# A two-block transformer kernel: who adds the experts' rows, who sums the squares, and the order of the modulation weights

## The chip, the cores and the metric

The kernel runs on one core of one Trainium2 chip. The metric is the device time of one execution in microseconds; three runs of the kernel before gave 2313.27, 2318.12 and 2326.68 us, so the median is 2318.12. The engines are called as in the profile: PE (TensorE's matmuls; PEld is its weight loads), DVE (VectorE), ACT (ScalarE), POOL (GpSimd) and SP (SyncE, which issues most DMAs).

## The reference

A sequence of 256 latent tokens and 256 context tokens, 1024 wide, goes through two blocks in float32. The first block has two layers. Each modulates the tokens, runs a mixer (an even one with neighbourhood attention and an mLSTM, then an odd one with grouped-query attention), adds its output to the residual `x`, and then runs 16 experts of which each token uses two:

```python
comb = (one_hot(e_idx, N_EXPERTS) * w[..., None]).sum(axis=1)
for e in range(N_EXPERTS):
    y = y + comb[:, e:e + 1] * ((silu(h @ w1[e]) * (h @ w3[e])) @ w2[e])
x = x + g2 * y                       # g2: a gate of the modulation
# the next layer begins with
h = x * rsqrt(mean(x * x) + EPS) * g * (1 + scale) + shift
# where shift, scale and gates are silu(c) @ ada_w[l] + ada_b[l]
```

In the first layer the experts run on all 512 tokens, in the second on the 256 latent tokens alone. The second block is two layers of a hybrid of attention and convolutions with a feed-forward part, on the latent tokens.

## The kernel before

The residual is kept feature-major: `xl` (latent) and `xc` (context) are tiles of 128 partitions x 8 groups (`k`) of features x 256 tokens. Every large product is made from three matmuls of halves: a weight tile `raw` is rounded on ACT into `wh` (L90), DVE subtracts to get `wl` (L91), and PE runs `wh` and `wl` against the halves of the input (L105 to L107). There are three buffers each for `wh` and `wl`, and eight for `raw`. SP loads the weights in the order in which the program asks for them.

**The end of an expert layer (`moe`, from L1689).** Each expert works on the up to 128 tokens that chose it. Experts 0 to 13 scatter their weighted rows to a DRAM tensor `yd` with one row for each token and choice (L1671, a DMA from POOL). When expert 14 has gone up, `rows_back` (L1692) loads these rows: for each block `t` of 128 tokens two tiles `g[0]`, `g[1]` in `raw` buffers, four blocks in the first layer and two in the second. Behind the last expert DVE adds each pair (L1732); an order written by hand (`issue_after`) puts these adds behind the last weight subtract, and the last one behind the last split of an expert's output. The outputs of experts 14 and 15 (`LATE` = 2) stay in SBUF as halves `yh`, `yl`. PE then builds for each `k` a bank of 256 or 512 tokens: matmuls of `yh`, `yl` with a selection matrix `which` (`late_sum`, L1743) and of the added rows with the identity, which transposes them (`first_sum`, L1737). DVE multiplies the bank by the gate and adds it to the residual (L1763), once for each `k` and segment: 16 instructions in the first layer, 8 in the second.

**The squares.** `Stats` collects the sum of squares of each token of the residual. In the first expert layer ACT squares two `k` of a segment at a time (`gather`, L187), DVE adds the squares of the pairs onto each other (L189) and the two halves of the result (L204), and PE sums over the partitions with a column of ones into `tot` (`settle`, L206). It settles twice: once when `k` = 5 is done, once at the end. The second expert layer only notes the tiles (`gather_later`), and the next block does the work. `Stats.add` (L213) is a method that no caller uses here: it squares on ACT and lets PE sum each square for itself; its tiles `sq` have three buffers. `Stats.rstd` (L228) takes mean and epsilon on DVE (L233), the power -0.5 on POOL (L168), and spreads the reciprocals over the partitions by matmuls with the identity (L239, "the spread").

**The next stage (`odd_mixer`, L1779).** It calls `rstd`, modulates both segments (L891 on DVE, L901 on ACT, L902 on DVE) and runs the first projection, `lin_tok` on four chunks of weights. Between chunks `c.between` is called, which runs one step of `ada`: matmuls of the second layer's modulation weights (L824) into a bank of the same PSUM pool as `tot`.

**Held splits.** `c.held` is a list from which `split_w` takes one entry at a time: the ACT cast and the DVE subtract of that weight tile are queued behind the two instructions of the entry. At the end of the first expert layer the first next tile is held behind the last row add and the last rounding of an expert's output (`c.early`), the two after it behind the last half add of squares and the last square. The order within each engine is otherwise made by a scheduler from priorities, when the program is built.

Of the kernel before, what the change touches and what calls it, by code (L numbers as in the profile page):

```python
# [170 lines left out]
class Stats:  # L171
# [41 lines left out]
    def add(self, i, x):  # L213

        c, nc = self.c, self.c.nc
        _, n, w = x.shape
        sq = c.const.tile([P, 512], F32, name="sq", tag="sq", bufs=3)
        sv = sq[:, :n * w].rearrange("p (n w) -> p n w", n=n)
        nc.scalar.activation(sv, x, AF.Square)
        for k in range(n):  # L220
            for t in range(w // P):
                left = self.left.get(i + t, KD) - 1
                nc.tensor.matmul(self.tot[:, i + t:i + t + 1], sv[:, k, t * P:(t + 1) * P], c.ones[:, 0:1],
                                 start=self.fresh, stop=left == 0, skip_group_check=True)
                self.fresh = False
                self.left[i + t] = left

    def rstd(self, i, n=1):  # L228

        c, nc = self.c, self.c.nc  # L230
        assert not any(self.left[i + j] for j in range(2 * n))
        r = c.const.tile([P, 4], F32, name="rstd", tag="rstd", bufs=2)
        nc.vector.tensor_scalar(r[:, :2 * n], self.tot[:, i:i + 2 * n], 1.0 / D, EPS, op0=ALU.mult, op1=ALU.add)  # L233
        c.rsqrt_small(r[:, :2 * n], r[:, :2 * n], 2 * n)
        outs = []
        for a in range(n):
            out = c.ps("rstd")
            for t in range(2):
                nc.tensor.matmul(out[:, t * P:(t + 1) * P], r[:, 2 * a + t:2 * a + t + 1].to_broadcast((P, P)), c.ident,  # L239
                                 start=True, stop=True, skip_group_check=True)  # L240
            outs.append(out[:, :256])
        return outs

# [1160 lines left out]
def moe(c, s, L, segs, mods, routes, yd, later, slots, late, more=()):  # L1404
# [287 lines left out]
    def rows_back():  # L1692

        for t in range(nt):
            g = []
            for k in range(2):
                g.append(c.raw().rearrange("p a b -> p (a b)"))
                nc.sync.dma_start(g[k], rows[t, :, k])
            gs.append(g)

    x, f = (xh, xl), None
# [25 lines left out]
                                            op0=ALU.add, op1=ALU.is_equal)  # L1727
    ys.append(down(NE - 1, *end))
    ys = ys[NE - LATE:]
    for g in gs:  # L1730
        with tc.issue_after(done[1].ins if g is gs[-1] else c.splits[-1]):
            added = nc.vector.tensor_tensor(g[0], g[0], g[1], op=ALU.add).ins  # L1732
    c.early = added, c.last_h

    def first_sum(k, ts):
        for t in ts:
# [11 lines left out]
    with tc.issue_after(done[0].ins):  # L1748
# [6 lines left out]
        for k in range(KD):  # L1755
# [4 lines left out]
            late_sum(k, (LATE - 1,))  # L1760
            ps = banks[k]
            for i, (x, r) in enumerate(segs):
                nc.vector.scalar_tensor_tensor(x[:, k, :], ps[:, 256 * i:256 * i + 256], mods.col(5, k, r), x[:, k, :],  # L1763
                                               op0=ALU.mult, op1=ALU.add)
            if k % 2:
                for i, (x, r) in enumerate(segs):
                    if later:
                        st.gather_later(x[:, k - 1:k + 1, :])
                    else:
                        place = spare([P, 512], F32, "sqs")  # L1770
                        q = st.gather(x[:, k - 1:k + 1, :], 2 * i, place)
                if k == KD - 3 and not later:
                    st.settle()
    if not later:
        c.held = [(st.settle().ins, q.ins)] * 2 + [c.early]
    return st


def odd_mixer(c, s, xl, xc, st, mods, A, B, ada):  # L1779
# [61 lines left out]
        nc.vector.tensor_tensor(B[:, :n, 1::2], x[:, :, 0::2], bc(tab[:, P + 1::2]), op=ALU.mult)  # L1841
        nc.vector.tensor_tensor(dst, A[:, :n], B[:, :n], op=ALU.add)

    c.between = lambda: ada(1)
    banks = [c.acc() for _ in range(4)]
    c.lin_tok(h, W[:, 1024:1536], 512, range(4), banks)
    for t in range(4):
        nc.scalar.copy(v[:, t, :], banks[t][:, 256:512])
        heads(banks[t][:, 0:256].rearrange("p (h d) -> p h d", d=P), 2, 1, t - 2 if t >= 2 else None, kk[:, t])
# [290 lines left out]
```

## Time and profile before

| | |
|---|---|
| median of three runs | 2318.12 us |
| profiled execution | 2316.98 us |
| its span | 2315.2 us |
| PE / PEld busy | 2222.4 us (96%) / 1887.8 us (82%) |
| DVE / ACT / POOL busy | 1789.7 us (77%) / 1505.2 us (65%) / 152.3 us (7%) |
| bytes moved by DMA | 507.24 MB |

The profile is one execution. Busy is the time in which an engine had an instruction running; a matmul's end is modelled, so a busy PE is not one at its peak. Instructions of one engine overlap a little in the records, so that steps are somewhat shorter than durations. PE's clock column is the share of full speed that was granted (1.00 is 2.4 GHz, 0.50 is 1.2 GHz). A wait is idle time of an engine in front of an instruction, with what released it.

### The profile page before, as it was taken

How to read it: one execution, taken by the hardware profiler on the slowest of the kernel's cores; microseconds unless marked ns; L12 is line 12 of the kernel's file. 1: busy time of each engine (PE TensorE's matmuls, PEld its weight loads, DVE VectorE, ACT ScalarE, POOL GpSimd, SP SyncE). 2: the span in 40 equal slices, each digit the busy share in tenths (PEclk: the TensorE clock that was granted, in tenths of full speed). 3: DMA queues.
4: the chain of work that ended last, by engine and by line, in shares of the span. 5: the costliest groups of instructions: out<-in, count | busy, mean ns of one | idle time of the engine just before them, and what ended most of it. 6: DMA issues, size and time to landing. Idle time of an engine off the chain costs nothing.

```text
span 2315.2 us, 37957 instructions
## 1 busy us (share of the span) xinstructions
PE 2222.4 (96%) x14089; PEld 1887.8 (82%) x14089; DVE 1789.7 (77%) x2817; ACT 1505.2 (65%) x2398; POOL 152.3 (7%) x202
## 2 busy tenths in 40 slices
PE   8999999889999998999999999999999999999999
PEld 5665657767777667777778899999999899999997
DVE  4334743789989775899888999778976899867984
ACT  4333442478877453788776999656765999755773
POOL 0020000111110100111101100000000100000000
PEclk9999979899999999999999999999999999999999
DMA  8577603899993745999946545656666645656653
GB/s 303 170 242 279 204 26 118 312 347 366 365 336 142 270 167 207 377 398 348 325 148 204 177 136 150 190 182 183 194 201 185 184 139 146 186 178 183 192 184 117
DMA packets 206204, 507.24 MB, mean 219 GB/s; under 512 B 22711, under 2 KB 32335, under 8 KB 206008
## 3 DMA queue, kind: packets, MB, share of 16 engines
q1 hardware_dynamic: 196728, 490.08, 63.1%
q0 software_dynamic: 9280, 14.62, 1.7%
q8 instruction: 114, 1.87, 0.3%
q14 instruction: 82, 0.67, 0.1%
HBM read 498.39 MB, written 25.19 MB: 226 GB/s over the span
## 4 chain that ended last, share of the span: by engine, by line
PE 51%; DVE 10%; issue 8%; ACT 6%; DMA 3%; POOL 1%; DVEq 0%; SPq 0%; ACTq 0%; POOLq 0%
PE acc L106 15%; PE acc L107 15%; PE acc L105 14%; DVE wl L91 6%; ACT wh L90 3%; PE ps L164 2%; ACT cp L592 1%; DMA raw<-in_exp_w 1%; DMA rawm<-in_exp_w 1%; PE ps L1903 1%; DMA rawr<-in_exp_w 1%; ACT mtf L1635 1%; PE ps L451 0%; PE acc L1894 0%; DVE conf L597 0%
## 5 line engine op out<-in xcount | busy, mean ns | idle before, releaser
L91 DVE TENSOR_TENSOR wl<-raw,wh 128x1024 fp32r<-128x1024 f32 (+2 forms) x520 | 616.1, 1191 | 240.8 <-ACT wh L90 236.4
L90 ACT CAST wh<-raw 128x1024 fp32r<-128x1024 f32 (+2 forms) x520 | 532.1, 1026 | 356.1 <-PE acc L106 187.4
L106 PE MATMUL acc<-hl,wh 128*128 128x256 f32 (+1 forms) x1568 | 450.0, 287 | 0.3 <-DVE hl L916 0.3
L107 PE MATMUL acc<-hh,wl 128*128 128x256 f32 (+1 forms) x1568 | 450.0, 287 | 0.0
L105 PE MATMUL acc<-hh,wh 128*128 128x256 f32 (+1 forms) x1568 | 449.1, 287 | 0.7 <-ACT hh L913 0.6
L105 PEld LDWEIGHTS acc<-hh,wh 128*128 128x128 f32 x1568 | 295.5, 189 | 11.7 <-issue 4.2
L106 PEld LDWEIGHTS acc<-hl,wh 128*128 128x128 f32 x1568 | 295.9, 189 | 7.0 <-issue 2.5
L107 PEld LDWEIGHTS acc<-hh,wl 128*128 128x128 f32 x1568 | 294.9, 188 | 5.8 <-issue 1.3
L91 DVE TENSOR_TENSOR wl<-rawm,wh 128x1024 fp32r<-128x1024 f32 x210 | 250.9, 1219 | 17.6 <-ACT wh L90 14.2
L90 ACT CAST wh<-rawm 128x1024 fp32r<-128x1024 f32 x210 | 218.1, 1052 | 48.8 <-PE acc L107 45.9
L106 PE MATMUL acc<-wl,xh 128*128 128x512 f32 x512 | 211.5, 413 | 16.4 <-DVE wl L91 16.1
L105 PE MATMUL acc<-wh,xh 128*128 128x512 f32 x512 | 202.0, 399 | 6.3 <-PEq L1328 6.3
L107 PE MATMUL acc<-wh,xl 128*128 128x512 f32 x512 | 202.5, 395 | 0.0
L105 PE MATMUL acc<-bh,wh 128*128 128x256 f32 x640 | 178.6, 279 | 0.7 <-ACT bh L273 0.7
L106 PE MATMUL acc<-bl,wh 128*128 128x256 f32 x640 | 178.7, 279 | 0.4 <-DVE bl L274 0.4
L107 PE MATMUL acc<-bh,wl 128*128 128x256 f32 x640 | 178.7, 279 | 0.0
L592 ACT ACTIVATE cp<-ap,col 128x256 f32<-128x256 f32 x368 | 164.7, 506 | 6.4 <-DVE conf L597 6.4
L106 PE MATMUL acc<-wl,hh 128*128 128x512 f32 (+1 forms) x384 | 145.4, 379 | 2.2 <-DVE wl L91 1.9
L105 PE MATMUL acc<-wh,hh 128*128 128x512 f32 (+1 forms) x384 | 147.1, 383 | 0.0
L106 PEld LDWEIGHTS acc<-wl,xh 128*128 128x128 f32 x512 | 97.1, 190 | 60.6 <-DVE wl L91 41.0
L107 PE MATMUL acc<-wh,hl 128*128 128x512 f32 (+1 forms) x384 | 144.6, 377 | 0.0
L106 PEld LDWEIGHTS acc<-bl,wh 128*128 128x128 f32 x640 | 121.1, 189 | 0.8 <-DVE bl L274 0.8
(493 smaller groups left out, 4514.4 us busy)
## 6 DMA issues: line engine op xcount, KB each, us to landing
rawm<-in_exp_w SPq DMA_DIRECT2D x210, 512.0 KB, 6.9
raw<-in_w_in SPq DMA_DIRECT2D x152, 512.0 KB, 3.6
raw<-in_exp_w SPq DMA_DIRECT2D x96, 512.0 KB, 7.0
raw<-in_ada_w SPq DMA_DIRECT2D x80, 512.0 KB, 5.1
raw<-in_w_up SPq DMA_DIRECT2D x80, 512.0 KB, 3.7
rawr<-in_exp_w SPq DMA_DIRECT2D x66, 512.0 KB, 7.0
raw<-in_w_down SPq DMA_DIRECT2D x44, 512.0 KB, 4.4
raw<-in_even_w_in SPq DMA_DIRECT2D x24, 512.0 KB, 5.1
```

What stands on the lines that cost most here:

```text
L90: nc.scalar.copy(h[:, :, :n], raw[:, :, :n])
L91: self.splits.append(nc.vector.tensor_tensor(l[:, :, :n], raw[:, :, :n], h[:, :, :n], op=ALU.subtract).ins)
L105: nc.tensor.matmul(out, a[0], b[0], start=start, stop=False, skip_group_check=True)
L106: nc.tensor.matmul(out, a[0], b[1], start=False, stop=False, skip_group_check=True)
L107: return nc.tensor.matmul(out, a[1], b[0], start=False, stop=stop, skip_group_check=True)
L164: self.nc.tensor.transpose(out, in_, self.ident[:n, :n])
L592: nc.scalar.activation(p[:, i, :], src[:, i, :], AF.Copy, scale=wv)
L1635: nc.scalar.activation(v, a, AF.Tanh, scale=0.5)
L1903: nc.tensor.matmul(po[:, :256], v[:, b, g0 * P:(g0 + 1) * P], pT[:, b].rearrange("p t q -> p (t q)"), start=b == 0, stop=b == 3)
```

## The change

The row pairs are added on POOL, in `rows_back`, right behind the loads of each pair, with no order by hand. The entry `c.early` names the last split of an expert's output in place of the last row add. In the first expert layer `Stats.add` takes the place of `gather` and `settle`: after each `k`, each segment is squared on ACT (128x256) and two matmuls sum it into `tot`, so there are 32 of these matmuls where there were 8. The two held tiles are now queued behind the last update of the residual and the last square. And the modulation steps that run between the four chunks of the first projection are queued on PE behind the last matmul of the spread.

```diff
@@ Stats.add
-        nc.scalar.activation(sv, x, AF.Square)
+        last = nc.scalar.activation(sv, x, AF.Square).ins
...
+        return last
@@ Stats.rstd
-                nc.tensor.matmul(out[:, t * P:(t + 1) * P], r[:, 2 * a + t:2 * a + t + 1].to_broadcast((P, P)), c.ident,
-                                 start=True, stop=True, skip_group_check=True)
+                self.spread = nc.tensor.matmul(out[:, t * P:(t + 1) * P],
+                                               r[:, 2 * a + t:2 * a + t + 1].to_broadcast((P, P)), c.ident,
+                                               start=True, stop=True, skip_group_check=True).ins
@@ moe, rows_back
                 nc.sync.dma_start(g[k], rows[t, :, k])
+            nc.gpsimd.tensor_tensor(g[0], g[0], g[1], op=ALU.add)
             gs.append(g)
@@ moe, behind the last expert
-    for g in gs:
-        with tc.issue_after(done[1].ins if g is gs[-1] else c.splits[-1]):
-            added = nc.vector.tensor_tensor(g[0], g[0], g[1], op=ALU.add).ins
-    c.early = added, c.last_h
+    c.early = done[1].ins, c.last_h
@@ moe, for each k
-                nc.vector.scalar_tensor_tensor(x[:, k, :], ps[:, 256 * i:256 * i + 256], mods.col(5, k, r), x[:, k, :],
-                                               op0=ALU.mult, op1=ALU.add)
-            if k % 2:
-                for i, (x, r) in enumerate(segs):
-                    if later:
-                        st.gather_later(x[:, k - 1:k + 1, :])
-                    else:
-                        place = spare([P, 512], F32, "sqs")
-                        q = st.gather(x[:, k - 1:k + 1, :], 2 * i, place)
-                if k == KD - 3 and not later:
-                    st.settle()
+                last = nc.vector.scalar_tensor_tensor(x[:, k, :], ps[:, 256 * i:256 * i + 256], mods.col(5, k, r),
+                                                      x[:, k, :], op0=ALU.mult, op1=ALU.add).ins
+            for i, (x, r) in enumerate(segs):
+                if not later:
+                    q = st.add(2 * i, x[:, k:k + 1, :])
+                elif k % 2:
+                    st.gather_later(x[:, k - 1:k + 1, :])
     if not later:
-        c.held = [(st.settle().ins, q.ins)] * 2 + [c.early]
+        c.held = [(last, q)] * 2 + [c.early]
@@ odd_mixer
-    c.between = lambda: ada(1)
+    def behind():
+        with c.tc.issue_after(st.spread):
+            ada(1)
+
+    c.between = behind
     banks = [c.acc() for _ in range(4)]
     c.lin_tok(h, W[:, 1024:1536], 512, range(4), banks)
+    c.between = lambda: ada(1)
```

## Rows read from the trace of the kernel before

**Rows 1.** The page's first part: busy us, share of the span, instructions.

```profile
PE 2222.4 (96%) x14089; PEld 1887.8 (82%) x14089; DVE 1789.7 (77%) x2817; ACT 1505.2 (65%) x2398; POOL 152.3 (7%) x202
```

**Rows 2.** Stretches: length; PE, PEld, DVE, ACT, POOL busy; clock; DMA share; GB/s.

```profile
735.00:745.00 10.00, 9.57 (x42) 7.53 (x43) 8.96 (x10) 6.26 (x8) 0.00 (x0) 1.00 0.77 296
...
751.00:760.50 9.50, 9.50 (x69) 8.82 (x69) 6.02 (x7) 2.31 (x3) 0.00 (x0) 1.00 0.65 195
760.50:766.40 5.90, 5.67 (x30) 4.26 (x28) 5.43 (x13) 2.31 (x4) 0.00 (x0) 1.00 0.38 138
766.40:771.20 4.80, 1.02 (x8) 0.97 (x8) 4.44 (x11) 2.29 (x5) 0.52 (x1) 0.88 0.96 341
771.20:773.10 1.90, 1.87 (x8) 1.78 (x8) 0.43 (x1) 1.89 (x3) 0.00 (x0) 0.50 1.02 385
...
779.10:795.50 16.40, 16.40 (x72) 13.35 (x72) 13.18 (x30) 7.65 (x15) 0.00 (x0) 1.00 0.71 241
...
1232.00:1240.00 8.00, 7.60 (x65) 7.31 (x63) 6.87 (x12) 3.94 (x7) 0.00 (x0) 1.00 0.53 145
```

**Rows 3.** Waits from 735 to 751: who for whom; us, times, longest.

```profile
PEld acc L106 <- DVE wl L91: 3.2, 5, 1.1
...
PE acc L106 <- DVE wl L91: 1.2, 2, 0.7
```

**Rows 4.** The row adds: ns min/median/max, first and last start; three in time order.

```profile
L1732 DVE TENSOR_TENSOR raw<-raw x6: 1215/1217/1221, 749.8 to 1233.7; 128x1024 f32<-128x1024 f32 x6
...
753.07 3.49 DVE L1732 TENSOR_TENSOR raw<-raw 128x1024 f32<-128x1024 f32 x3
```

**Rows 5.** The rows' loads: issue ns, first and last start, landing.

```profile
L1698 SPq DMA_DIRECT2D raw<-yd x12: 319/382/597, 730.0 to 1216.0; - x12
...
DMA to landing us min/median/max: 3.7/5.6/8.1
```

**Rows 6.** POOL's groups: count, busy us, mean ns of one, idle before.

```profile
L168 POOL TENSOR_TENSOR oqm<-oqm,mhalf 128x4 f32<-128x4 f32 x4 | 4.0, 1007 | 24.3 <-DVE oqm L1822 24.3
L1810 POOL TENSOR_TENSOR turn<-rope2d,ogqk 128x256 f32<-128x256 f32 x2 | 1.6, 776 | 0.0
...
L1811 POOL TENSOR_TENSOR turn<-rope2d,ogqk 128x128 f32<-128x128 f32 x2 | 1.0, 507 | 0.0
```

**Rows 7.** Time order (start, us); L902: ns min/median/max of three from 778.

```profile
773.19 2.36 DVE L91 TENSOR_TENSOR wl<-raw,wh 128x1024 fp32r<-128x1024 f32 x2
773.36 1.96 POOL L168 TENSOR_TENSOR rstd<-rstd,mhalf 128x4 f32<-128x4 f32 x1 [2.65 <-DVE rstd L233]
...
778.20 0.70 POOL L1812 TENSOR_TENSOR turn<-rope2d,ogqk 128x128 f32<-128x128 f32 x1
...
L902 DVE SCALAR_TENSOR_TENSOR hl<-nt,mod,hh x3: 472/480/739, 778.1 to 779.1; 128x256 fp32r<-128x256 f32 x3
```

**Rows 8.** DVE in time order during the last experts of the first layer.

```profile
734.09 3.49 DVE L91 TENSOR_TENSOR wl<-rawm,wh 128x1024 fp32r<-128x1024 f32 x3
738.21 1.11 DVE L1637 TENSOR_TENSOR mtf<-mtf,acc 128x512 f32<-128x512 f32 x1 [0.63 <-PE acc L107]
...
747.58 2.35 DVE L91 TENSOR_TENSOR wl<-rawm,wh 128x1024 fp32r<-128x1024 f32 x2
```

**Rows 9.** Time order from the first update of the residual to the projection.

```profile
760.97 0.48 DVE L1763 SCALAR_TENSOR_TENSOR xc<-ps,mod,xc 128x256 f32<-128x256 f32 x1 [3.27 <-PE ps L1743]
...
764.50 1.29 DVE L189 TENSOR_TENSOR sqs<-sqs 128x512 f32<-128x512 f32 x2
...
769.94 0.47 DVE L1763 SCALAR_TENSOR_TENSOR xl<-acc,mod,xl 128x256 f32<-128x256 f32 x1
...
773.33 1.92 PE L824 MATMUL ada<-raw,cs 128*32 128x512 f32 x2 [0.25 <-DVE rstd L233]
775.37 1.85 PE L239 MATMUL rstd<-ident,rstd 128*128 128x128 f32 x8
777.16 1.92 PE L824 MATMUL ada<-raw,cs 128*32 128x512 f32 x16
```

## The prediction

> **What bounds the kernel now.** I began with the page's busy line: PE is busy 96% of a span of 2315.2 us [rows 1]. Then I read a table of stretches around the end of the first expert layer (735 to 795 us), because the diff touches only the ends of the two expert layers and the first 15 us behind the first one. The reader is to see three things in it [rows 2]. While the last experts run (735 to 745), DVE is busy 8.96 of 10 us, PE 9.57. From 751 to 766.4 PE has no gap but 0.23 us. From 766.4 to 771.2 PE does 1.02 us of work, and from 771.2 on it is granted half the clock; from 779.1 PE is full again (16.40 of 16.40). So the only slack that the change can collect lies between 766.4 and 779, about 12 us or 0.5% of the span, and a gain anywhere else needs PE to stop waiting. The list of waits shows where PE waits before that: on the subtract `wl` of DVE (L91), 3.2 + 1.2 us within 16 us [rows 3]. DVE therefore has almost no reserve in that stretch.
>
> **Part 1, the row-pair adds.** Removed from DVE: four adds of 1.217 us behind the first expert layer and two behind the second [rows 4]. The first begins at 749.8, the other three of the first layer fill 753.07 to 756.56 [rows 4], when PE has a closed row of other sums to work off; in the second layer, where the last begins at 1233.7, PE is busy 7.60 of the 8 us from 1232 [rows 2]. Taking them off DVE is worth nothing on PE, and I book 0; it could be 0.5 us if a sum of the last row block came late somewhere.
>
> Added on POOL: the same six adds, each waiting only for its two rows of `yd`. Issue begins at 730.0, a row block lands within 3.7 to 8.1 us [rows 5], so in the first layer they can start between about 735.5 and 741.5, in the second, with the last issue at 1216.0, up to about 1221. That is during the last experts, before DVE's old place for them. No row shows an add of this size on POOL. From below: DVE's own 1.22 us [rows 4]. From the nearest POOL rows: 128x256 takes 0.776, 128x128 takes 0.507 us [rows 6], 2.1 ns more for each further column, so 1024 columns give 0.776 + 768 x 0.0021 = 2.4 us; these rows read some operands strided, and I take 2.2. Alone, four of them need 9 us and would be done by about 747, before PE's sums begin at 751 [rows 2]. Behind them on POOL stands the next stage's clearing of `yd` and the power at 773.36 [rows 7], in the second layer memsets and rope tables of the next block, so the POOL queue itself costs nothing.
>
> What costs is the other engine. The reciprocal's power on POOL takes 1.007 us [rows 6], but 1.96 us when it begins at 773.36 while DVE is in two `wl` subtracts from 773.19 on: it ended about 1.0 us after the first of them ended [rows 7]. The opposite also shows: of three DVE instructions `hl` beside POOL's table products, two take 0.47 to 0.48 us and one 0.739, while the POOL product of 128x128 that begins at 778.20 takes 0.70 instead of 0.507 [rows 6, 7]. So an instruction of either engine that reads two SBUF tiles waits for the other's. With a POOL instruction of half a microsecond DVE lost 0.26; what it loses to one of 2.2 us no row shows. Lower end: 0, where POOL's reads find DVE idle or reading from PSUM. Upper end: the 2.2 us each. Ten `wl` subtracts lie in the stretch from 734.09 to 749.93, at a step of 1.14 us (3.49 us for three at its start, 2.35 for two at its end) [rows 8]; nine of them, 10.3 us, come behind the first landing at about 735.5, and with four adds of 2.2 that makes 19 us of exclusive work in 14.4, so if the hold is a full one, about 5 us must come out as delay, and PE has nothing but the `wl` to wait for [rows 3]. In the second layer, with two adds, one can start beside a DVE instruction that reads PSUM, as the 1.11 us at 738.21 [rows 8], and hold the next subtract for half its length or so, the other for most of it: 2 us. I take +5 and +2, since the row with 0.739 against 0.48 shows DVE waiting for nearly all that the POOL instruction spends on its columns. Ends: 0 and 6 x 2.2 = 13.
>
> The Trainium skill has this as a rule ("SBUF — State Buffer", section "Who interferes with whom"): a DVE instruction with two SBUF inputs and a GpSimd instruction that reads SBUF share one port pair as an exclusive lock, and whichever comes second is blocked to the other's end. By that rule the hold is the whole add, and the full upper end is a rival below; the trace agrees for POOL behind DVE (1.96 against 1.007) and shows the other direction for short instructions alone. The skill's "GPSIMD Engine Reference", section "Elementwise — side-by-side cycle accounting", gives 4497 ns for an add of 2048 columns; half of that, an estimate of 2.25 us, would leave the sum as it is.
>
> The second row buffer of each pair comes back earlier, so SP can load the next weights from about 740 instead of 751. PE is never short of weights from 779 to 795 [rows 2], so this buys 0.
>
> **Part 2, squares by PE alone.** Before: 16 updates on DVE of 0.48 us, overlapped to a step of 0.39, the first at 760.97 and the last at 769.94, with four adds of squares (two of them 1.29 us) and two half adds between [rows 9]: 769.94 - 760.97 - 15 x 0.39 = 3.1 us that go. The update chain alone would end at 767.3. But PE cannot follow. Each k and segment now takes two matmuls, which the trace shows as two records each: 8 x 2 x 2 x 2 = 64 records instead of 16. Eight of them took 1.02 us in the stretch granted 0.88 of the clock, and 1.87 in the one at 0.50 [rows 2], so about 0.12 each: 7.7 us. PE is closed to 766.4, so its last square ends at about 766.4 + 7.7 = 774.1, where the second batch of eight now ends at about 773.1 [rows 2]. +1.0. It can be +0.3 if a record takes 0.11, or +4 if PE, in order, also waits at each k for a step of DVE (8 x 0.39 = 3.1). ACT has three buffers for squares instead of spare places, so its last squares follow PE's pace, and the casts that are held behind the last square do too.
>
> What comes back: with PE busy up to there, I expect the higher clock to last. The spread of eight records takes 1.85 us at 775.37, where the granted clock is about half; the first eight sums took 1.02 [rows 2]: -0.8. The power on POOL takes 1.96 because of the `wl` pair [rows 7]; whether these subtracts move ahead of it or stay beside it hangs on ACT's last square: -0.95 or 0, I take -0.5.
>
> **Part 3, modulation weights behind the spread.** Now two records of them (one matmul) run from 773.33 to 775.25, in the shadow of the power, and 16 from 777.16, before the first projection matmul [rows 9]. Moving the two behind the spread costs 2 x 1.92 / 16 = 0.25 us; it protects the spread only if the power gets shorter than 1.9. The wait is on PE's own queue, so nothing waits for it that the spread didn't stop already. For the three later chunks the order is past the spread anyway: 0.
>
> **Sum.** Part 1 +5 +2, part 2 +1.0 -0.8 -0.5, part 3 +0.25: about +7 us on the profiled execution's 2316.98 us (span 2315.2 and 1.8 around it), so 2324. That execution is 1.1 us below the median of the three runs, 2318.12, which themselves lie between 2313.27 and 2326.68; I add nothing for it. About 0.5%, 11.6 us, is what a measurement of this kernel can tell from no change; my +7 (0.3%) is below that.
>
> **The rivals.**
> A, the adds hide: POOL takes its turns while DVE reads PSUM or idles, and gives way otherwise. For it: from 773.19 DVE's two subtracts kept 1.18 us each beside the power [rows 7]. Against it: the 0.739, and a DVE busy 9 of 10 us. Then part 1 is 0 and the rest is about 0, at best -2 (short power, high clock, 0.11 a record): 2315 to 2317.
>
> B, the full hold: each add blocks a subtract for all its 2.2 us and PE waits for each. 6 x 2.2 = 13, rest 0: 2330, slower by 0.5%. It decides from the point where no add finds DVE in a PSUM read. For it: PE waits for `wl` seven times within 16 us [rows 3]. Against: DVE instructions that read PSUM lie between, one of them 1.11 us [rows 8]. (This is what the rule of the Trainium skill's page "SBUF — State Buffer", named above, would make of it.)
>
> C, the adds starve until DVE's last subtract (749.9) and come at 752, 754, 757 and 759, where DVE now has the last by 756.56 [rows 4]: up to +2.6 in the first layer, less in the second, so 2320. This stays in my range.
>
> D, PE stalls at each square: +4 on top of the forecast, 2328.
>
> **Chances.** Forecast with C and D 0.57, A 0.25, B 0.15, 0.03 for an order of instructions that differs more widely. The range takes in A's low end less the spread of the runs (2315 - 3) and B with part 2's upper end (2330 + 3): 2312 to 2333. Forecast alone: 2318 to 2329. Faster by over 0.5% has no case but the last: 0.03. Slower by over 0.5%: 0.1 from B, 0.07 from the high end of the forecast with D: 0.17. Within 0.5%: 0.80.
>
> **What would show it.** Part 1 is right if POOL's adds are above 2.2 us by their waits, some `wl` of the last expert is above 1.3 us, PE's wait on `wl` there rises from 4.4 to about 9 us, and PE's sums, which now begin at 751, begin at about 756. If no `wl` is longer, A holds. Part 2 is right if PE is closed to about 774 plus that shift, with 64 records of `tot` and the clock above 0.9 there; wrong if PE shows gaps behind ACT's squares. Part 3: no modulation matmul before the spread, and a spread of about 1 us. A time below 2310 would mean that the tail behind the first expert layer gave over half its 12 us, for which no term here stands.

## The result, and the profile after

The changed kernel takes 2339.62 us (median of 6 runs, 2333.94 to 2347.18), the kernel before beside it 2317.80 (6 runs, 2313.27 to 2326.68): ratio 1.0106, interval 1.0082 to 1.0131. (The ratios on record are not the quotients of the two medians; that of these is 1.0094.) The changed kernel is slower by about 1%, 21.8 us between the medians. The prediction had 2324, held a change of that size to be below what a measurement can tell, and gave 2333 as its upper end. The profiled execution took 2339.07 us, its span is 2337.3. Two of the runs below fell far out, one of e2 (10692.55 us) and one of e4 (2743.90 us); they are left out of the ratios and move the medians given by less than 1 us.

The page's first part, which stands against [rows 1]:

```profile
PE 2235.2 (96%) x14137; PEld 1901.6 (81%) x14137; DVE 1788.2 (77%) x2803; ACT 1507.6 (65%) x2406; POOL 170.3 (7%) x208
```

PE has 48 matmul records more (64 records of sums of squares in place of 16; each sum is two records) and POOL six instructions. PE's busy time grew by 12.8 us, more than 48 short records are worth (about 6 us at 0.12 each). So some of PE's work probably ran slower.

**Where the time went.** Both traces hold the same GpSimd instructions of the stages around the change. I compared their start times and read how the distance between the two kernels grows from one landmark to the next. The landmarks and their start times:

```
landmark (GpSimd instruction)                    before   changed
last scatter of the first expert layer            726.77    722.88
power of the reciprocals                          773.36    781.36
first `ms` power of the next stage                799.63    810.03
a gather, start of the second expert layer        949.54    959.00
a scatter, start of the second expert layer      1031.94   1046.32
a gather, end of the second expert layer         1109.08   1123.43
an `rs` power of the next block                  1304.13   1323.46
```

The four stretches in which the changed kernel loses:

```
stretch                             lost, us
first layer's end, to the power     11.9
from the power into the projection   2.4
start of the second expert layer     4.9
second layer's end                   5.0
```

That is 24.2 us; in the rest, where nothing was changed, single executions of every kernel drift by some us either way (ahead of 726.77 the changed kernel is 3.9 us early, another execution 12.3 us late). The step in the start of the second expert layer lies at a place that the prediction never looked at.

**The row adds.** The group of the adds and that of the subtracts (ns min/median/max, first and last start), then POOL and DVE in time order, against [rows 4] and [rows 8]:

```profile
L1701 POOL TENSOR_TENSOR raw<-raw x6: 2457/3370/3439, 732.0 to 1235.9; 128x1024 f32<-128x1024 f32 x6
...
L91 DVE TENSOR_TENSOR wl<-rawm,wh x210: 1201/1220/3445, 419.8 to 1245.9; 128x1024 fp32r<-128x1024 f32 x105
...
732.03 12.81 POOL L1701 TENSOR_TENSOR raw<-raw 128x1024 f32<-128x1024 f32 x4 [8.17 <-DMA raw<-yd]
...
730.22 5.71 DVE L91 TENSOR_TENSOR wl<-rawm,wh 128x1024 fp32r<-128x1024 f32 x3
...
736.84 5.76 DVE L91 TENSOR_TENSOR wl<-rawm,wh 128x1024 fp32r<-128x1024 f32 x2
743.12 3.94 DVE L91 TENSOR_TENSOR wl<-rawm,wh 128x1024 fp32r<-128x1024 f32 x2
```

While POOL has its four adds in hand (732.03 to 744.84), three subtracts take 5.71 instead of 3.49 and two take 5.76 instead of 2.35; single ones reach 3.445 us. PE waits for them. The list of waits from 722 to 760, against [rows 3]:

```profile
PEld acc L106 <- DVE wl L91: 10.9, 9, 2.1
...
PE acc L106 <- DVE wl L91: 7.3, 7, 1.7
```

PE's own 7.3 us stood at 1.2 in the window of [rows 3], and at 1.4 in one as long as this. These 5.9 us more are most of the delay of the first late sum, which begins at these times before and in the changed kernel:

```profile
751.29 0.40 PE L1743 MATMUL ps<-which,yh 128*128 128x512 f32 x1
...
753.93 0.40 PE L1743 MATMUL ps<-which,yh 128*128 128x512 f32 x1
```

Counted from the last scatter it begins after 31.05 us instead of 24.52, that is 6.5 us later.

**The squares.** Stretches from the first late sum on; the columns are those of [rows 2]:

```profile
753.90:763.40 9.50, 9.50 (x69) 8.81 (x68) 2.64 (x3) 1.98 (x3) 0.00 (x0) 1.00 0.20 55
763.40:767.50 4.10, 4.10 (x26) 3.61 (x25) 3.89 (x10) 1.95 (x5) 0.00 (x0) 1.00 0.00 0
767.50:769.80 2.30, 2.30 (x21) 2.30 (x20) 1.69 (x5) 1.72 (x5) 0.00 (x0) 0.92 0.00 0
769.80:775.50 5.70, 5.70 (x24) 5.45 (x25) 0.00 (x0) 1.59 (x5) 0.00 (x0) 0.50 0.37 107
775.50:781.00 5.50, 5.50 (x26) 5.36 (x24) 0.88 (x2) 2.29 (x5) 0.00 (x0) 0.50 1.03 398
781.00:783.40 2.40, 0.08 (x1) 0.00 (x0) 1.33 (x2) 0.00 (x0) 2.04 (x2) 0.50 1.19 393
783.40:787.70 4.30, 4.29 (x18) 2.27 (x18) 2.66 (x7) 1.42 (x3) 3.24 (x6) 0.64 0.83 307
```

The column behind the five busy times is the granted clock. From 769.8 it is 0.50 (1.2 GHz) although PE is busy for 5.70 of 5.70 and then 5.50 of 5.50 us. What PE does there, in time order:

```profile
767.49 2.50 PE L223 MATMUL tot<-ones,sq 128*128 128x1 f32 x20
...
775.97 5.11 PE L223 MATMUL tot<-ones,sq 128*128 128x1 f32 x24
...
783.41 2.07 PE L240 MATMUL rstd<-ident,rstd 128*128 128x128 f32 x8 [2.33 <-POOL rstd L168]
785.41 2.42 PE L826 MATMUL ada<-raw,cs 128*32 128x512 f32 x10
```

A record of a sum costs 0.125 us at 767.49 and 0.21 at 775.97. From the first late sum (753.93) to the power (781.36) it takes 27.4 us, where the kernel before took 22.1 (751.29 to 773.36): 5.4 us more. The spread is not shorter (2.07 against 1.85 [rows 9]), and ahead of it PE now stands for 2.33 us, where the kernel before did two modulation records.

**A branch.** The second layer's step of 4.9 us, PE in time order:

```profile
970.06 0.48 PE L105 MATMUL acc<-wh,xh 128*128 128x512 f32 x1
974.75 0.79 PE L106 MATMUL acc<-wl,xh 128*128 128x512 f32 x1 [4.21 <-issue]
975.34 0.63 PE L107 MATMUL acc<-wh,xl 128*128 128x512 f32 x1
```

"issue" means that PE waited for nothing which the profile shows: no engine's result and no load is named. It happens one matmul behind the place (L1330) where all engines test a flag and jump over the code for overfull experts. Behind it the matmuls take 0.63 us for a while in place of 0.39; that makes the 4.2 us to 4.9. In the trace of before no matmul has an "issue" wait.

### The profile page after: what moved, and what is told of

It reads as the page before. It is cut to its first block, busy times and chain, and to the rows that moved or that the text cites. A ratio compares the mean times of both kernels' runs of the same rounds, so it can differ in the third digit from the quotient of the medians.

```text
span 2337.3 us, 38065 instructions
## 1 busy us (share of the span) xinstructions
PE 2235.2 (96%) x14137; PEld 1901.6 (81%) x14137; DVE 1788.2 (77%) x2803; ACT 1507.6 (65%) x2406; POOL 170.3 (7%) x208
## 4 chain that ended last, share of the span: by engine, by line
PE 44%; ACT 6%; DVE 6%; issue 2%; POOL 0%; DMA 0%; DVEq 0%; ACTq 0%
PE acc L106 14%; PE acc L107 14%; PE acc L105 13%; DVE wl L91 3%; ACT wh L90 2%; ACT cp L594 2%; PE ps L164 1%; PE ps L453 0%; DVE conf L599 0%; ACT ta L497 0%; POOL rs L168 0%; ACT mtf L1637 0%; PE ps L511 0%; PE ps L488 0%; DVE sq L189 0%
## 5 line engine op out<-in xcount | busy, mean ns | idle before, releaser
L105 PEld LDWEIGHTS acc<-hh,wh 128*128 128x128 f32 x1568 | 295.1, 188 | 11.9 <-issue 4.2
L91 DVE TENSOR_TENSOR wl<-rawm,wh 128x1024 fp32r<-128x1024 f32 x210 | 259.6, 1261 | 17.2 <-ACT wh L90 13.7
```

The costliest lines, as they stand in the source:

```text
L91: self.splits.append(nc.vector.tensor_tensor(l[:, :, :n], raw[:, :, :n], h[:, :, :n], op=ALU.subtract).ins)
L105: nc.tensor.matmul(out, a[0], b[0], start=start, stop=False, skip_group_check=True)
```

## The experiments

Each stood beside runs of the kernel before on the same chip. "Step" is the growth between landmarks as in the table above, from one profiled execution each; ratios are against the kernel before, with their interval.

### The three parts alone

**e1_pool_adds**: the adds alone.

```diff
+            nc.gpsimd.tensor_tensor(g[0], g[0], g[1], op=ALU.add)
-            added = nc.vector.tensor_tensor(g[0], g[0], g[1], op=ALU.add).ins   # behind the splits
```

> The kernel before with part 1 alone: the six row adds on POOL as the rows land, squares and modulation order as before. Theory H (an add on POOL and a subtract of DVE with two SBUF inputs exclude each other for the whole instruction): the adds take 2.4 to 3.5 us, four to six subtracts of the last experts are longer than 2 us, PE's sums begin some 6.5 us later in the first layer and some 3 to 5 us later in the second; +10 to +12 us, ratio about 1.005. Rival O (what cost time in the changed kernel is the tail behind the first expert layer and instructions in another order elsewhere): no more than +3 us here.

Measured: 2327.81 us, ratio 1.0056 (1.0033 to 1.0079). Steps: 5.7 us at the first layer's end, 6.4 at the second's, 0.0 at the start of the second layer. The groups from 700 to 800 (busy, mean ns):

```profile
L91 DVE TENSOR_TENSOR wl<-rawm,wh 128x1024 fp32r<-128x1024 f32 x17 | 26.6, 1595 | 0.1
...
L1699 POOL TENSOR_TENSOR raw<-raw 128x1024 f32<-128x1024 f32 x4 | 14.0, 3522 | 8.1 <-DMA raw<-yd 8.1
```

The adds alone lengthen the subtracts and cost about half of the loss.

The 6.4 us of the second layer are not the adds' alone. They split at the power of the next block's reciprocals: 4.8 ahead of it (3.3 in the changed kernel), and 1.6 right behind it, where the granted clock falls. The 3.2 us behind that power, in the kernel before and in the changed one:

```profile
1253.20:1256.40 3.20, 3.15 (x27) 3.15 (x28) 2.00 (x6) 1.82 (x4) 0.00 (x0) 1.00 0.57 174
...
1270.90:1274.10 3.20, 3.14 (x15) 3.14 (x16) 1.64 (x5) 1.17 (x3) 0.01 (x1) 0.54 0.64 186
```

All six kernels with the adds as the rows land lose 1.4 to 1.6 us there, but so do e2, e4 and e9, which have no add on POOL, while e3, e8, e11, e13 and e15 lose nothing (e14 0.5). PE waits 1.40 us for the power in either case; what decides whether the clock falls stays open.

**e2_pe_squares**: the squares alone, adds and modulation as before (`st.add` for each k and segment in place of `gather` and `settle`).

> The kernel before with part 2 alone: squares on ACT for each k and segment and 32 matmuls of one column, row adds on DVE and modulation order as before. Theory C (the matmuls of one column let the granted clock fall to 0.50 although PE never idles, and the bank sums queued among them run at half speed too): clock 0.50 from about 8 us behind the first update on, tot complete 5 to 6 us later than before, +5 to +6 us in all, ratio about 1.002. Rival P (the matmuls simply add their own 7 us to a closed PE, as forecast): clock above 0.9 up to the end of the squares, tot at most 1.5 us later.

Measured: 2330.89 us, ratio 1.0060 (1.0034 to 1.0085). Steps: 5.7 at the first layer's end, 0.7 behind the power, 5.3 at the start of the second layer, 1.7 at its end (the fall of the clock named under e1), and no subtract of `rawm`, the experts' weights, above 1.24 us. The loss among the squares and the wait behind the branch appear here without any add on POOL.

**e3_ada_order**: the modulation order alone (`ada(1)` behind `st.spread`).

> The kernel before with part 3 alone: the modulation steps of the first four chunks behind the spread on PE. All theories: no modulation matmul between tot and the spread, at most 0.5 us either way, ratio 1.000. A rival that puts the loss of the changed kernel on this order expects +2 us or more up to the end of the first projection.

Measured: 2328.23 us, ratio 1.0035 (1.0011 to 1.0059). PE in time order and the stretches around it:

```profile
778.22 2.08 PE L239 MATMUL rstd<-ident,rstd 128*128 128x128 f32 x8 [2.30 <-POOL rstd L168]
780.23 4.44 PE L825 MATMUL ada<-raw,cs 128*32 128x512 f32 x18
...
776.10:780.20 4.10, 1.98 (x8) 1.78 (x8) 2.78 (x4) 0.12 (x1) 4.00 (x5) 0.50 1.05 407
780.20:784.60 4.40, 4.40 (x20) 0.90 (x19) 4.27 (x11) 2.60 (x6) 1.35 (x3) 0.61 0.91 301
```

In the kernel before, the stretch of the 16 modulation records behind the spread [rows 9]:

```profile
777.10:779.10 2.00, 2.00 (x19) 0.51 (x17) 1.85 (x5) 1.42 (x3) 1.81 (x3) 1.00 1.06 400
```

In e3 PE stands still for 2.30 us ahead of the spread, and the 18 modulation records behind it take 4.44 us at a clock of 0.61, where 16 took 1.92 at 1.00. The step is 2.8: the expectation of at most 0.5 was wrong, that of the rival right. All five kernels with this part have 2.4 to 2.8 there, the ten others 0.0 to 1.4. The other 5 us of this ratio can't be put down to the order. The interval reaches down to 1.0011, which is about the step. In the profiled execution 4.6 us come between 800 and 950 us, in the attention stage, where the clock was 0.51 from 846 to 852 and in the kernel before did not fall; but e13, which has the old order, loses 4.2 us there with such a fall, and the changed kernel, which has the new one, loses nothing there.

The three ratios add up to 1.5%, more than the 0.8 to 1.3% of the whole change: e3's 5 us are in that sum, and the fall of the clock behind the next block's power is in it twice.

### The clock

**e4_pe_squares_wide**: e2 with 128 columns of ones in each sum in place of one.

```diff
-  nc.tensor.matmul(self.tot[:, i + t:i + t + 1], sv[:, k, t * P:(t + 1) * P], c.ones[:, 0:1], ...)
+  nc.tensor.matmul(self.tot[:, (i + t) * P:(i + t + 1) * P], sv[:, k, t * P:(t + 1) * P], c.ones, ...)
```

> As the kernel with part 2 alone, but each of the 32 matmuls of squares multiplies by 128 columns of ones in place of one (tot gets 128 equal columns for each block of tokens, of which one is read): the same number of matmuls and weight loads. Theory C: the clock stays at 1.00 to the end of the squares, the step stays at 0.11 us a record, tot is complete 4 to 6 us earlier than in the kernel with one column, and the time is that of the kernel before or up to 2 us less. Rival P: no change against one column, or slower by what 128 columns cost.

Measured: 2325.79 us, ratio 1.0034 (1.0010 to 1.0057). The step at the first layer's end falls from 5.7 to 1.6; the ones at the start of the second layer (5.1) and at its end (1.6) stay, so the time stays above that of the kernel before, where no more than its time was expected. A stretch of the sums in e2:

```profile
768.50:774.50 6.00, 6.00 (x26) 5.71 (x27) 0.00 (x0) 1.67 (x4) 0.00 (x0) 0.50 0.38 112
```

and in e4:

```profile
766.00:774.50 8.50, 7.29 (x53) 6.12 (x51) 2.62 (x7) 3.70 (x8) 0.00 (x0) 1.00 0.30 83
```

PE is busy for 6.00 of 6.00 us in the first and for 7.29 of 8.50 in the second, and it is the second that keeps 2.4 GHz. The same 64 sums with more columns are cheaper.

**e5_after_wide**: the whole change with that width.

> The whole change, but each matmul of the squares has 128 columns of ones in place of one (the same squares, the same sums, only the width of what moves). Theory (the granted clock): the one-column matmuls let it fall to 0.50 while TensorE is busy, so here it stays at 1.00 from the first late sum to the first projection matmul; first late sum to the reciprocal's start 22 to 23 us instead of 27.2, spread of 8 in about 1.1 us instead of 2.07. The holds of the high/low subtracts (about +6 us in each layer) and the 4.2 us wait for nothing visible in the second layer stay. In all about 6 us under the changed kernel: 2331 to 2335, ratio to the kernel before about 1.007. Rival (the late start of the sums alone, through the row adds, makes the tail long): the tail stays at 27 us and the time at 2340, 1.010.

Measured: 2336.04 us, ratio 1.0090 (1.0064 to 1.0115). The step at the first layer's end is 8.0 instead of 11.9; behind it 2.5, 5.0 and 5.0 as in the changed kernel. The clock stays at 1.00 among the sums, and 3.9 us of the 11.9 are gone. Of the 8.0 that are left, 6.5 stand ahead of the first late sum (the holds of the subtracts) and 1.5 behind it (the length of the sums).

The two wide kernels, which differ in the adds and in the modulation order, also show part 3 at work. The spread in e4, where two modulation records run ahead of it, and in e5, where they don't:

```profile
776.73 1.16 PE L242 MATMUL rstd<-ident,rstd 128*128 128x128 f32 x8 [1.05 <-POOL rstd L168]
...
779.38 2.08 PE L242 MATMUL rstd<-ident,rstd 128*128 128x128 f32 x8 [2.35 <-POOL rstd L168]
```

Both came out of their sums at 1.00. Behind a wait of 1.05 us the spread takes 1.16, behind one of 2.35 it takes 2.08, and the clock is down.

**e13_before_wide**: the kernel before with that width in its eight sums.

> The kernel before, where the eight sums of squares by TensorE in front of the reciprocals have 128 columns of ones in place of one; the rest as it is. If the one-column matmuls bring the clock down, the granted clock stays above 0.5 until the projection and the spread of 8 takes about 1.1 us instead of 1.85: -1 to -2 us at 800 us, in the time about 0.9995. If the clock falls there because TensorE waits for VectorE (the two waits of 1 to 2 us ahead of the sums), the clock is 0.50 as before and the time the same or 0.5 us longer.

Measured: 2323.21 us, ratio 1.0015 (0.9992 to 1.0039), not told apart from no change. The stretch of the sums:

```profile
764.00:768.80 4.80, 3.29 (x16) 2.75 (x16) 3.89 (x9) 3.03 (x4) 0.52 (x1) 0.64 1.02 389
```

There PE waits 2.65 and 0.94 us for VectorE ahead of the sums, and the clock falls in spite of the width: the second of the two cases expected.

### The wait behind the branch

PE's branch instruction in the kernel before (ns min/median/max over the two layers, the first layer's being the long one):

```profile
L1328 PEldq COMPARE_BRANCH  x2: 333/3310/6288, 469.2 to 959.2; - x2
```

The trace lists program transfers of PE, 16 KB each: in four intervals of the trace of before, 249 to 253 matmuls and weight loads (and a few semaphore instructions) are executed between two of them; in others it is more or fewer, as the transfers come late. I take a block as 256 instructions. Transposes, which are never executed, were put into the first layer's overfull-expert code, so that only the place of what follows changes:

```diff
     ps = bank()
+    for t in range(N if L == 0 else 0):
+        c.transpose(ps[:NE, 0:P], rest[:, 0, :])
```

**e7_after_page** (the changed kernel, N = 16), **e8_before_page** (the kernel before, N = 23) and **e9_before_pads** (the kernel before with 48 tiny matmuls at its start):

> The changed kernel with 16 more transposes inside the first layer's overflow branch, which is not taken: nothing more is executed, but what follows stands 32 instructions later in TensorE's program. Theory (program supply): the changed kernel has 46 more TensorE instructions ahead of the second layer's branch than the kernel before (24 matmuls with their weight loads, two semaphore instructions fewer), so the block of instructions that holds the branch's target ends 2 instructions behind it and the next block has to come first; here the target stands in the next block's beginning, the wait of 4.2 us at L106 behind the branch goes, and the time falls by about 5 us against the changed kernel: 2334 to 2336, ratio about 1.008. Rival (the wait is for an expert weight or for VectorE, through the changed order of loads): the wait of 4.2 us stays and the time too, 2339, 1.010.

> The kernel before with 23 more transposes inside the first layer's overflow branch, which is not taken, so that the second layer's branch and its target stand at the places that they have in the changed kernel; nothing else differs and nothing more is executed. Theory (program supply): the 4.2 us wait at L106 right behind the second layer's branch appears, with matmuls at the lower clock behind it, +5 us from that place on: about 2323, ratio 1.002. Rival (the wait comes with the squares or with the order of loads): no such wait, 1.000.

> The kernel before with 48 matmuls of one column by one on the constant ones at the very start, while TensorE waits for the context rows (its first instruction starts at 6.25 us); 96 more instructions stand ahead of both branches. Theory (program supply): in the first layer the branch now jumps into the block next to its own, so its 6.3 us fall to 0.4 or at most 1; the second layer's stays short: -5 to -6 us from 476 us on, about 2313, ratio 0.9975. The start may lose up to 1 us. Rival (the first layer's branch waits 6 us for its flag's register or for the queue of loads, wherever it stands): 6.3 us as before, ratio 1.000 to 1.0005.

Measured: e7 2340.80 us, 1.0126 (1.0102 to 1.0149); e8 2314.02, 0.9999 (0.9976 to 1.0023); e9 2316.82, 1.0009 (0.9984 to 1.0035). All three expectations failed, and by their numbers the rivals came true: e7 kept a step of 5.0, e8 has none, e9's first branch still takes 6.4 us, and its second took 4.6. But the traces show more than the numbers. PE's branch instruction in e7:

```profile
L1330 PEldq COMPARE_BRANCH  x2: 5914/5926/5939, 481.9 to 984.9; - x2
```

and in the changed kernel:

```profile
L1330 PEldq COMPARE_BRANCH  x2: 333/3100/5868, 465.8 to 968.7; - x2
```

Sixteen transposes that nobody executes turned a branch of 0.33 us with a wait of 4.2 behind it into one of 5.9 us without. So the place in the program matters, and my count of it was wrong: a float32 matmul that is no transpose is two matmuls and two weight loads in the trace. The 24 matmuls that the change puts ahead of the second layer's branch are 96 instructions, with two semaphore instructions fewer 94, not 46. The traces hold 9158 records of PE ahead of that branch in the changed kernel and 9064 before.

Counted anew, the second layer's branch stands so. The jump goes over 346 instructions of the program; one offset, the same for all kernels, is fitted (so that in the changed kernel a block ends 4 instructions behind the jump's target):

```
kernel        branch at   target: block, place   branch us   wait behind it
before            68      next, 158              0.33        none
after            162      next, 252              0.33        4.2
e7               194      next but one, 28       5.91        none
e8               114      next, 204              0.33        none
e9                 4      next, 94               4.58        none
```

By this count a target in the next block cost nothing where that block had had time to come (in e9, where the branch stands 4 instructions into its own, 4.6 us); one further on had to be fetched, 5.9 us; and with the target at a block's very end PE waited for the block behind it: in the changed kernel's trace a program transfer runs from 972.34 to 973.40, inside the wait of 970.5 to 974.75. In the first layer the skipped code is 662 instructions or more in every kernel, so the target is never in the next block, and every branch there took 5.9 to 6.4 us, before as after. That this has the same cause is inferred; no run shortened it.

**e10_after_dead81** (the changed kernel, N = 81: by the new count the places of the kernel before) and **e11_before_dead47** (the kernel before, N = 47: the places of the changed kernel):

> The changed kernel with 81 more transposes in the first layer's overflow branch, which is not taken; nothing more is executed. The count is mended: a float32 matmul is four TensorE instructions in the trace (two matmuls with their weight loads), so the change puts 94 instructions ahead of the second layer's branch, not 46, and 81 transposes (162 instructions) make that 256, one block of the program, which is what the intervals between two program transfers hold. Theory (program supply): branch and target stand in their blocks as in the kernel before, so the branch takes 0.3 us, no wait of 4 us follows, and the time falls by about 5 us against the changed kernel, 2333 to 2336, ratio 1.007 to 1.009. Rival (the wait comes with the squares or the order of loads): the 4.2 us wait or a 6 us branch stays, ratio 1.010.

> The kernel before with 47 more transposes in the first layer's overflow branch, which is not taken: 94 instructions, by the mended count the shift of the changed kernel. Theory (program supply): the wait of about 4.2 us at L106, behind the first matmul behind the second layer's branch, appears with nothing else changed; +5 us from there on, about 2320 where the kernel before has 2315, ratio 1.002. Rival: no such wait, 1.000.

Measured: e10 2343.45 us, 1.0088 (1.0055 to 1.0121); e11 2321.99, 1.0019 (0.9995 to 1.0043). The medians can't tell 5 us; the traces can. PE behind the branch in e10:

```profile
980.24 0.47 PE L105 MATMUL acc<-wh,xh 128*128 128x512 f32 x1
980.86 0.47 PE L106 MATMUL acc<-wl,xh 128*128 128x512 f32 x1
```

and in e11:

```profile
959.35 0.47 PE L105 MATMUL acc<-wh,xh 128*128 128x512 f32 x1
964.00 0.80 PE L106 MATMUL acc<-wl,xh 128*128 128x512 f32 x1 [4.18 <-issue]
```

The wait is gone from the changed kernel (step 0.1 instead of 4.9) and has come into the kernel before (step 6.1 instead of 0), with no executed instruction changed in either. These two were forecast from the new count, which the five kernels of the table had been used to make. The Trainium skill ("Runtime: NRT & Kernel Launch", section "Instruction fetch mechanics") says that programs are fetched in blocks of 256 instructions, each while the one before it runs, and that a taken branch whose target lies outside the two blocks at hand waits for a fetch; these runs agree, with 5.9 us for it. Of the step from one block into the next the same section of the Trainium skill says that its cost is "mostly hidden"; behind this branch it was not, 4.2 us.

**e14_squares_mended**: e4 with N = 81.

> Squares by TensorE alone, with 128 columns of ones, row adds on VectorE, modulation where the kernel before has it, and 81 more transposes in the first layer's overflow branch that is not taken. If the clock and the program supply are the two whole costs of this part of the change, nothing is left but the 1.3 us by which the reciprocals began later in the wide form: no 4 us wait behind the second layer's branch, 2316 to 2318, ratio 1.0005. Rival (a third cost, an order of loads or of buffers that the removed scratch tiles changed): still 4 us or more, 1.002 and above.

Measured: 2317.95 us, ratio 1.0008 (0.9987 to 1.0029); steps 1.5, 0.4, 0.1, 0.6. By the steps, squares on PE cost little beyond the clock, the program's blocks and the 1.5 us of their length; the interval of the ratio alone would still allow 6.7 us.

### Hold or slow engine

**e12_pool_adds_late**: the adds given to POOL at the place in the program where DVE had them.

> The kernel before with its row adds on GpSimd, but at the place where VectorE had them, behind the last high/low subtracts, and not as the rows land. Theory (GpSimd and VectorE hold each other where both read two operands from SBUF): no subtract above 1.3 us beside them, the adds take 2.2 to 2.6 us each, the late sums begin as in the kernel before; the adds end about 5 us later than VectorE's did, and TensorE waits 0 to 3 us for them: ratio 1.000 to 1.0015. Rival (GpSimd's slowness is what costs, wherever the adds stand): +6 us as in the kernel with the adds as the rows land, 1.003 and more.

Measured: 2326.04 us, ratio 1.0040 (1.0018 to 1.0063), steps 6.5 and 5.8. It didn't test what it was meant to: POOL's queue is empty there, so a later place in it holds nothing back.

```profile
730.37 12.84 POOL L1732 TENSOR_TENSOR raw<-raw 128x1024 f32<-128x1024 f32 x4 [8.11 <-DMA raw<-yd]
```

The adds ran as the rows landed, and this is e1 once more.

**e15_pool_adds_behind**: each add held back by data.

```diff
+            nc.vector.tensor_copy(g[1][:, 0:1], g[1][:, 0:1])      # where DVE had its add
-            added = nc.vector.tensor_tensor(g[0], g[0], g[1], op=ALU.add).ins
+            added = nc.gpsimd.tensor_tensor(g[0], g[0], g[1], op=ALU.add).ins
```

> The kernel before with its row adds on GpSimd, each held back by a VectorE copy of one column of the row's second half, which stands where VectorE's add stood (behind the splits). Theory (each engine holds the other where both read two operands from SBUF): the subtracts of the last two experts stay at 1.22 us, the first late sum does not move, the adds alone take 2.2 to 2.6 us and end about 5 us later than VectorE's did, TensorE waits 0 to 3 us for them: ratio 1.000 to 1.0015. Rival (GpSimd's slowness costs wherever the adds stand): +6 us, 1.0025 and more.

Measured: 2319.13 us, ratio 1.0019 (0.9996 to 1.0042). POOL's adds in time order, their group, and the subtracts:

```profile
748.14 2.40 POOL L1733 TENSOR_TENSOR raw<-raw 128x1024 f32<-128x1024 f32 x1 [22.33 <-DVE raw L1732]
751.35 7.97 POOL L1733 TENSOR_TENSOR raw<-raw 128x1024 f32<-128x1024 f32 x3 [0.81 <-DVE raw L1732]
...
L1733 POOL TENSOR_TENSOR raw<-raw x6: 2352/2383/3326, 748.1 to 1235.1; 128x1024 f32<-128x1024 f32 x6
...
L91 DVE TENSOR_TENSOR wl<-rawm,wh x210: 1201/1221/1234, 422.0 to 1230.4; 128x1024 fp32r<-128x1024 f32 x105
```

Apart, an add takes 2.35 to 2.40 us, and no subtract of the last experts is above 1.24. The one add of 3.33 lies beside the one weight subtract that still meets it (1.82 us). The first late sum begins where the kernel before has it (749.34, in an execution that is 1.94 us early at the scatter; 751.29 before). PE then waits 0.40 and 1.31 us for the adds, and the steps are 2.2 and 2.5 in place of 5.7 and 6.4 (4.8 without the fall of the clock, which e15 does not have). More than half of the adds' cost was the two engines' meeting, the rest is POOL's pace.

No experiment points to a version that beats the kernel before; the best forms (e14, e15) can't be told from it.

## Why the prediction was wrong

**Part 1, the adds: right in kind, the second layer too small.** The prediction took 2.2 us for an add, +5 us for the first layer and +2 for the second. An add alone is 2.4 us. The first layer lost 6.5 in the changed kernel, 5.7 in e1 and 6.5 in e12, near the term, and by the route that the prediction named: longer subtracts, PE's wait for `wl` up, the late sums later. (The sign that it gave, 4.4 to about 9 us of wait, added the waits of PE's matmuls and of its weight loads, which lie in the same gaps; the matmuls' own went from 1.4 to 7.3.) The second layer lost 5.0 to 6.6 in the six kernels that have the adds as the rows land. The step that failed is "the other for most of it: 2 us". In e1's trace the two adds hold two subtracts for 5.04 us instead of 2.35, which is 2.7; a further subtract (of the next block's weights, 1.22 us) then falls among the updates of the residual, and up to the power 4.8 us are lost, 3.3 in the changed kernel. The last 1.4 to 1.6 us are the fall of the clock behind the power, which the prediction did not have and which kernels without these adds show too. The rule of the Trainium skill ("SBUF — State Buffer", section "Who interferes with whom"), an exclusive lock between the two engines, was weighed as rival B. The traces agree with it now in both directions (3.4 us beside, 1.2 and 2.4 apart); rival B's 13 us are close to the 12.1 and 12.3 that the steps of e1 and e12 add up to, in part by luck, since 1.6 of each are that fall of the clock.

**Part 2, the squares: the step that failed is "with PE busy up to there, I expect the higher clock to last".** It booked +1.0 for length, -0.8 for the spread and -0.5 for the power; the runs show +5.7 in e2 and +5.4 in the changed kernel. A busy PE did not keep the clock: it fell to 0.50 among sums of one column and stayed at 1.00 among sums of 128 (e4), with the step then at +1.6, close to the +1.0. The spread took 1.16 us there in place of 1.85, near the -0.8, but the stretch from the power into the projection was 0.4 us longer all the same. Why sums of one column lose the clock, the runs do not show. The rows of the kernel before could not tell: it was granted 0.50 at its own second eight sums [rows 2], but behind gaps of PE, and there it falls with 128 columns too (e13). The power stayed at 1.99 us, since one subtract of DVE stayed beside it (1.23 us from 781.23).

**Part 3, the modulation: the step that failed is "in the shadow of the power".** The price was booked as the length of two records, 0.25 us. They also kept PE at work; without them it stood 2.3 us, and the spread and the modulation behind it ran at the lower clock: 2.4 to 2.8 us.

**Missing from the sum: 4.9 us of program supply.** The prediction counted only the time of the 48 added records, not that they move everything behind them in PE's program. None of the rows read before the change gave that price. A row that is not among them hints at the kind: the first layer's branch already takes 6.3 us in the kernel before.

**The sum.** 7 us predicted; by steps 11.9 + 2.4 + 4.9 + 5.0 = 24.2, measured 21.8. Of the difference of 17, about 4.5 belong to the adds (1.5 in the first layer, 3.0 in the second, and of these 1.6 to the clock behind the power), 5.7 to the squares (3.9 of it the clock, by e5), 2 to the modulation and 5 to the branch. The direction was the sum's own. The chances followed its size, which lay below what can be measured, and neither the clock among the sums nor the branch had an upper end in the range.

## What to carry to other kernels

Count an offload to GpSimd at its own time plus what it takes from VectorE while both read SBUF, unless a data dependence keeps them apart; a later place in GpSimd's program did not (e12), since its queue was empty. Read the granted clock among short matmuls, not PE's busy share, before work is moved there, and price a removed filler by the clock that it kept up. Where a kernel has a branch that PE takes, compare the branch's duration and the "issue" wait behind it whenever PE's instruction count ahead of it changes: a few microseconds come and go with the program's length alone.

## What the runs showed of the hardware that was not expected

PE, busy for all of two stretches of 5.70 and 5.50 us by the profile, was granted 0.50 of the clock, with sums of one column among wider matmuls. A taken branch on PE costs 0.33, 4.6 or 5.9 us, or 0.33 with 4.2 behind it, by its place in the program. The first layer's branch costs every version, the kernel before too, 5.9 to 6.4 us; a jump short enough to land in the next block might save that, which was not tried.
